# An instruction scheduler that models the vector engines' queues, in a one-layer hybrid decoder step

## The chip, the cores and the metric

The kernel runs on one core of one Trainium2 chip. The metric is the device time of one execution in microseconds (us), given as the median of several runs. One core has a matrix engine (TensorE, in the profile PE; PEld is its weight load), a vector engine (VectorE, DVE), an activation engine (ScalarE, ACT), a general engine (GpSimd, POOL) and a queue that issues transfers (SyncE, SP). Each engine works through its own instructions in the order in which the program lists them, and instructions on different engines wait for each other by semaphores.

## The reference

The reference is one step of one decoder layer for a prompt group (512 tokens) and a sample group (8 sequences of 8 tokens with 1024 cached positions each). Both share the weights.

```
h = rmsnorm(x, norm1_w)
rq, rk, rv, rg, aq, ak, av = split(h @ w_in)          # 7 sections of 512 columns
ro = silu(rg) * (groupnorm(retention(rq, rk, rv, state)) * gn_w + gn_b)
ao = dilated_attention(aq, concat(cache_k, ak), concat(cache_v, av))   # softmax, 8 heads of 64
x  = x + concat(ro, ao) @ w_out
h  = rmsnorm(x, norm2_w)
ua, ub = split(h @ w_up)                              # 2 x 2816 columns
x  = x + (silu(causal_conv3(ua)) * ub) @ w_down
y  = rmsnorm(x, normf_w)
```

It also returns the retention states, the new key and value windows and the convolution states of both groups. All arrays are float32.

## The kernel before, in words

All 576 tokens (512 prompt, 64 sample) are kept transposed, with the model's 1024 columns on partitions in 8 tiles. A dense layer is computed in chunks of 128 output columns. A chunk is 8 steps of 6 matmuls: activations and weights are split into a high and a low part (`xhi`/`xlo`, `whi`/`wlo`), three products are summed, and each covers the 576 tokens in two halves of 288. ScalarE makes `whi` from the loaded `wraw` (line 219), VectorE makes `wlo` (line 229), and `dense` (lines 245 to 261) issues the steps (line 254).

There are three stretches. In the first, the inputs are transposed and normalised and the retention heads run beside the input projection. In the middle one, after retention has ended, both attentions run beside what is left of the input projection. In the last one come the output projection and the gated convolution FFN.

The order of the instructions is made by the program itself, when it is built. Each part of the work is a Python generator, a stream. `Merge` (lines 96 to 143) keeps a clock in modelled nanoseconds of TensorE. A stream issues some instructions and then yields `(c0, c1)`: how long TensorE will be busy with them, and how long from then on the stream is not to be resumed (a guess written by hand at each yield, for the work of the other engines). It may yield `None` when it can't go on. Streams with a `left` (an estimate of their TensorE time still to come) share the matrix engine in proportion, by a virtual time `vt`; a third number in the yield is charged in place of `c0`. Streams without `left` go first whenever their time has come. There are three with `left` in the middle stretch: `in_proj` (the input projection), `attn_prompt` and `attn_sample`.

The middle stretch in detail. A head pair `hp` (0 to 3) needs the chunks of sections 5 (keys), 4 (queries) and 6 (values) of the input projection; `in_post` multiplies each finished chunk by `rstd_b` (lines 557 and 563) and transposes keys and values (`natural`, line 496). After all head pairs come four chunks of section 3, the gates (line 527).

`attn_prompt` starts four units per head pair (`attn_unit`), with at most two in flight: scores (lines 766 to 771), bias and minimum on VectorE (779), exponential on ScalarE (786), reciprocal of the sum on VectorE (789), scaling on GpSimd (791), transposes of the scaled weights (797), copies out of PSUM (801), product with the values (810).

`attn_sample` runs eight units, two per head pair, each of four sequences. Before a unit, the keys of each sequence are transposed (`keys`, lines 883 and 884, six transposes and two copies). When all four are there and the head pair's sections are there, GpSimd copies the new tokens' keys in (line 982) and `unit` is started: scores (893), bias and minimum (900), exponential (905), reciprocal and scaling (907, 908), transposes (916, 917), copies (920, 921), product with the cached values (928), copy (937), transpose (943), copies into `aoT` (946). Cached values lie in six buffers: after the third key of the next unit the stream waits for the current unit to have used its values (`while len(V) > 5`, line 975).

PSUM is shared: four small tiles `m` and two large tiles `d`. `room(n)` and `give(n)` count the small tiles in use; `give` frees them at once when the reading instruction has been issued. The large tiles are used by `in_proj` for its chunks and by `unit`, twice, for scores and for transposes. Nothing in the program counts them; a matmul that writes to a tile whose last reader has not finished waits on the engine. The input projection waits for the attention in one place (line 582): a chunk of head pair 2 or 3 is started only when all six attention units of head pair 0 or 1 are done.

Of the kernel before, what the change touches and what calls it, by code (L numbers as in the profile page):

```python
# [10 lines left out]
F32 = mybir.dt.float32  # L11
# [3 lines left out]
OP = mybir.AluOpType  # L15
# [3 lines left out]
P = 128  # L19
D = 1024  # L20
NP = 512
# [4 lines left out]
TS = 8  # L26
# [66 lines left out]
    return {"c_ident": ident.astype(f), "c_small": small, "c_kdec": kdec, "c_pbias": pb, "c_sbias": sb.astype(f)}  # L93


class Merge:


# [2 lines left out]

    def __init__(self):
        self.clock, self.live, self.n = 0.0, [], 0

    def floor(self):
        return min([e["vt"] for e in self.live if e["left"] and not e["stuck"]], default=0.0)

    def add(self, gen, left=None, delay=0.0):  # L110
        self.n += 1
        self.live.append({"g": gen, "left": left, "vt": self.floor(), "at": self.clock + delay, "n": self.n,
                          "stuck": False})

    def run(self, until=None):
        while self.live and not (until and until()):
            free = [e for e in self.live if not e["stuck"]]
            assert free, "every stream waits"
            ok = [e for e in free if e["at"] <= self.clock]
            if ok:  # L120
                e = min(ok, key=lambda e: (e["left"] is not None, e["vt"] if e["left"] else e["at"], e["n"]))
            else:
                e = min(free, key=lambda e: (e["at"], e["n"]))
                self.clock = e["at"]
            try:
# [12 lines left out]
            self.clock += c[0]  # L138
            e["at"] = self.clock + c[1]
            if e["left"]:  # L140
                p = c[2] if len(c) > 2 else c[0]
                e["vt"] += p / e["left"]
                e["left"] = max(e["left"] - p, 2000.0)
# [2 lines left out]
@with_exitstack  # L146
def decoder_step(ctx, tc, a):
    nc = tc.nc
    pe, dve, act, pool, sp = nc.tensor, nc.vector, nc.scalar, nc.gpsimd, nc.sync
# [11 lines left out]

    def room(n):

        while held[0] + n > 4:
            yield None
        held[0] += n

    def give(n):
        held[0] -= n

    def dtile():
        return psd.tile([P, 1024], F32, name="d", tag="d")

    def f32(ap):
        return ap.bitcast(F32)
# [149 lines left out]
    def halves():  # L325
        return [(h2, slice(h2 * 64, h2 * 64 + 64)) for h2 in range(2)]

    mg = Merge()
# [193 lines left out]
    def in_post(m, ps):  # L522
        sec, hp = m // 4, m % 4
        y = tok(ps)
        if sec == 3:
            t = atp.tile([P, T], F32, name="t3", tag="t6", bufs=1)
            dve.tensor_mul(t, y, rstd_b)
            yield 0.0, 800.0
            act.activation(t, t, AF.Silu)
            yield 0.0, 1700.0  # L530
            while ret_done[0] <= hp:
                yield None
            (dve if hp == 3 else pool).tensor_tensor(roT[:, hp], roT[:, hp], t, op=OP.mult)
            ready.add(hp)
        elif sec < 4:
            while sec == 1 and hp not in kready:
                yield None
            r = R.setdefault(hp, {})
            t = rp.tile([P, T], F32, name=f"r{sec}", tag=f"r{sec}", bufs=2)
            dve.tensor_mul(t, y, kds.pop(hp) if sec == 1 else rstd_b)  # L540
            if m in first:
                evac.append(m)
            while not psm:
                yield None
            yield 0.0, 700.0
            if sec in (1, 2):
                n = rp.tile([P, 5, P], F32, name=f"n{sec}", tag=f"n{sec}", bufs=2)
                yield from natural(t, n, slice(0, NS))
                r["kv"[sec - 1]] = n
            if sec == 1 and hp < 3:  # L550
                mg.add(load_kdec(hp + 1))
            r[sec] = t
        else:
            r = A.setdefault(hp, {})
            t = atp.tile([P, T], F32, name=f"t{sec}", tag=f"t{sec}", bufs=1 if sec == 6 else 2)
            if sec == 4:
                dve.scalar_tensor_tensor(t, y, -(DH ** -0.5), rstd_b, op0=OP.mult, op1=OP.mult)  # L557
                yield 0.0, 2300.0
                for h2, q in halves():
                    pool.tensor_copy(qbs[hp % 2][q, :, h2 * TS:(h2 + 1) * TS],  # L560
                                     t[q, NP:].rearrange("p (b t) -> p b t", b=B))
            else:
                dve.tensor_mul(t, y, rstd_b)
                yield 0.0, 1700.0
                n = atp.tile([P, 5, P], F32, name=f"n{sec}", tag=f"n{sec}", bufs=1 if sec == 5 else 2)
                if sec == 6:
                    pool.memset(n[:NS, 4], 0.0)
                yield from natural(t, n, UP)
                if sec == 6:
                    r["v"] = n  # L570
            r[sec] = t
            if sec > 4:
                yield 0.0, 3100.0
                store_window(n, "k" if sec == 5 else "v", hp)

    def in_proj():
        for m in IN_ORDER:
            sec, hp = m // 4, m % 4
            if m in first:
                ps = first[m]  # L580
            else:
                while hp > 1 and (sec < 3 and ret_done[0] < hp - 1 or sec > 3 and used.get(hp - 2, 0) < 6):
                    yield None
                ps = dtile()
                for c in dense(ps, ("in", m, 0), xhis, xlos, 0, KD, True, True):
                    yield c
                    if m == IN_ORDER[-1]:
                        last_in.append(1)
# [155 lines left out]
    def attn_unit(hp, i):  # L744
# [42 lines left out]
        yield 0.0, 600.0  # L787
        for ps, s, c in S:
            dve.reciprocal(c[:, 2:3], c[:, 1:2])  # L789
        for ps, s, c in S:  # L790
            pool.tensor_scalar(s[:, :n], s[:, :n], c[:, 2:3], 1.0, op0=OP.mult, op1=OP.mult)  # L791
        yield 0.0, 2.5 * n + 300.0
        yield from room(2)
        for ps, s, c in S:
            ps = mtile()
# [60 lines left out]
    def attn_sample():  # L856
# [19 lines left out]
        def keys(u, x):  # L876
            hp, g = units[u]
            b = 4 * g + x
            kt = kvb[0].tile([P, SK], F32, name="kt", tag="kt", bufs=5)
            for w in range(2):  # L880
                ps = mtile()
                for j in range(3):
                    pe.transpose(ps[:, j * P:(j + 1) * P], K[u, x][:, 3 * w + j], ident)  # L883
                (act.copy if w else dve.tensor_copy)(kt[:, w * 384:w * 384 + 384], ps[:, :384])  # L884
            del K[u, x]
            KT[u, x] = kt

        def unit(u):
            hp, g = units[u]
            ps = dtile()  # L890
            for n0, n1_ in ((0, 512), (512, SK)):
                for x in range(4):
# [2 lines left out]
            for x in range(4):  # L895
# [3 lines left out]
            c = kvb[0].tile([P, 4], F32, name="ssc", tag="ssc", bufs=2)  # L899
            dve.tensor_tensor_reduce(out=s[:, :SK], in0=ps[:, :SK], in1=SB[hp], scale=1.0, scalar=3e38, op0=OP.add,  # L900
                                     op1=OP.min, accum_out=c[:, 0:1])
            if g == 1 and hp < 3:
                load_bias(hp + 1)
            yield 0.0, 700.0
# [6 lines left out]
                              s[:, None, KEYS:SK].to_broadcast([P, B, TS]),  # L911
                              mine[:, g, :, None].to_broadcast([P, B, TS]), op=OP.mult)
            yield 0.0, 1100.0
            ps = dtile()
            for j in range(6):
                pe.transpose(ps[:, j * P:(j + 1) * P], s[:, j * P:(j + 1) * P], ident)
# [2 lines left out]
            pt = kvb[0].tile([P, 7, P], F32, name="spt", tag="spt", bufs=1)  # L919
            dve.tensor_copy(pt[:, :3].rearrange("p j q -> p (j q)"), ps[:, :384])  # L920
            act.copy(pt[:, 3:7].rearrange("p j q -> p (j q)"), ps[:, 384:KEYS + P])
            yield 0.0, 2200.0
            yield from room(1)
            ps = mtile()
# [42 lines left out]
        for u in range(8):  # L967
            hp, g = units[u]
            for x in range(4):
                yield from room(2)  # L970
                keys(u, x)
                give(2)
                yield 660.0, 1600.0
                ahead(4 * u + x + 4, "k")
                while len(V) > 5:
                    yield None
# [13 lines left out]
    fin_ret = []  # L990

# [28 lines left out]

    mg.add(mix_split())
    mg.run()
    mid.close()


# [306 lines left out]
```

## Time and profile before

| what | value |
|---|---|
| median of 3 runs | 830.26 us (829.99 to 830.6) |
| profiled execution, device time | 830.02 us |
| its span, first to last instruction | 828.2 us |
| PE busy | 809.3 us (98%) |
| PEld busy | 772.3 us (93%) |
| DVE, ACT, POOL busy | 413.4, 294.4, 148.0 us |
| granted TensorE clock | 0.997 of full speed |

A matmul's record lasts from its start to its last result, and the next one starts before that; so neighbouring matmuls overlap in the trace, and a PE that is shown busy may still have lost a fraction of a matmul. An engine's idle time before an instruction is put down to what ended it: another engine's instruction, a transfer, or "issue", where the profile shows nothing that it waited for.

### The profile page before, as it was taken

The numbers are of one execution on the slowest core, as the hardware profiler recorded it, in microseconds if no ns is written. First come the engines' busy times: TensorE is split into PE (matmuls) and PEld (weight loads), VectorE is DVE, ScalarE is ACT, GpSimd is POOL, SyncE is SP. The second block draws the span as 40 slices with busy tenths as digits, with TensorE's granted clock in tenths as the row PEclk, the third lists the DMA queues.
The fourth block names the chain that finished last, engine by engine and source line by source line (L and its number), as shares of the span: only waits on it lengthen the run. The fifth ranks groups of instructions, "written<-read, shape, count | busy, mean of one in ns | idle before, by whom it ended". The sixth has DMA issues, their size and how long they took to land.

```text
span 828.2 us, 15913 instructions
## 1 busy us (share of the span) xinstructions
PE 809.3 (98%) x6559; PEld 772.3 (93%) x6559; DVE 413.4 (50%) x792; ACT 294.4 (36%) x503; POOL 148.0 (18%) x240
## 2 busy tenths in 40 slices
PE   7999999999999999999999999999999999999995
PEld 5999999887887888999999999999999999999995
DVE  4664555665546566743545545432245545443333
ACT  5422222454535567433223323311123323332222
POOL 1321202111110213032122322100012322310111
PEclk9999999999999999999999999999999999999998
DMA  9354753678786863456255554443334455543213
GB/s 265 105 175 115 213 173 101 184 210 226 213 254 185 228 177 91 111 185 197 77 179 178 178 187 160 124 137 91 96 99 161 145 153 179 172 160 93 71 52 115
DMA packets 179798, 128.67 MB, mean 155 GB/s; under 512 B 14976, under 2 KB 176400, under 8 KB 179213
## 3 DMA queue, kind: packets, MB, share of 16 engines
q1 hardware_dynamic: 178573, 93.75, 40.4%
q10 hardware_dynamic: 928, 33.63, 11.3%
q8 instruction: 52, 0.85, 0.4%
q0 software_dynamic: 224, 0.28, 0.1%
q14 instruction: 21, 0.17, 0.1%
HBM read 121.52 MB, written 39.66 MB: 195 GB/s over the span
## 4 chain that ended last, share of the span: by engine, by line
PE 93%; ACT 3%; DVE 1%; issue 1%; DMA 1%; POOL 0%; SPq 0%; ACTq 0%; DVEq 0%
PE d L254 74%; PE m L883 2%; PE d L451 2%; PE m L928 1%; PE d L893 1%; PE m L810 1%; PE m L797 1%; PE m L496 1%; PE m L1222 1%; PE px L254 1%; PE m L666 1%; DMA wraw<-in_w_in_dram 1%; ACT s L786 1%; PE m L630 1%; PE px L410 1%
## 5 line engine op out<-in xcount | busy, mean ns | idle before, releaser
L219 ACT ACTIVATE whi<-wraw 128x1024 fp32r<-128x1024 f32 (+2 forms) x114 | 110.5, 970 | 369.2 <-issue 182.6
L229 DVE TENSOR_TENSOR wlo<-wraw,whi 128x1024 fp32r<-128x1024 f32 (+2 forms) x114 | 127.1, 1115 | 121.7 <-ACT whi L219 118.9
L254 PE MATMUL d<-bhi,whi 128*128 128x288 f32 x768 | 172.7, 306 | 1.2 <-DVE t L557 1.2
L254 PE MATMUL d<-bhi,wlo 128*128 128x288 f32 x768 | 164.2, 295 | 0.0
L254 PE MATMUL d<-blo,whi 128*128 128x288 f32 x768 | 163.9, 295 | 0.0
L254 PE MATMUL d<-hhi,whi 128*128 128x288 f32 x704 | 151.0, 296 | 0.0
L254 PE MATMUL d<-hlo,whi 128*128 128x288 f32 x704 | 150.8, 296 | 0.0
L254 PE MATMUL d<-hhi,wlo 128*128 128x288 f32 x704 | 150.7, 296 | 0.0
L254 PEld LDWEIGHTS d<-bhi,whi 128*128 128x128 f32 x768 | 121.7, 189 | 6.3 <-issue 3.1
L254 PEld LDWEIGHTS d<-bhi,wlo 128*128 128x128 f32 x768 | 123.3, 188 | 0.0
L254 PEld LDWEIGHTS d<-blo,whi 128*128 128x128 f32 x768 | 123.2, 188 | 0.0
L254 PEld LDWEIGHTS d<-hhi,whi 128*128 128x128 f32 x704 | 113.5, 189 | 0.1
L254 PEld LDWEIGHTS d<-hhi,wlo 128*128 128x128 f32 x704 | 113.5, 189 | 0.0
L254 PEld LDWEIGHTS d<-hlo,whi 128*128 128x128 f32 x704 | 113.5, 189 | 0.0
L1130 DVE TENSOR_TENSOR ue<-d,rstd_b 128x512 f32<-128x512 f32 x22 | 15.2, 691 | 74.5 <-PE d L254 74.5
L1149 POOL TENSOR_TENSOR g<-g,cv 128x512 f32<-128x512 f32 x20 | 25.8, 1289 | 142.2 <-DVE g L1146 136.7
L791 POOL TENSOR_SCALAR s<-s,sc 128x128 f32<-128x128 f32 (+3 forms) x32 | 17.3, 549 | 140.5 <-DVE sc L789 125.9
L1046 POOL TENSOR_TENSOR acc<-acc,sq 128x576 f32<-128x576 f32 x13 | 20.9, 1611 | 104.2 <-ACT sq L1045 104.2
L1135 POOL COPY cout<-ue 128x2 f32<-128x2 f32 x22 | 5.7, 260 | 137.6 <-DVE ue L1130 137.6
L884 ACT COPY kt<-m 128x384 f32<-128x384 f32 x32 | 15.3, 479 | 38.4 <-PE m L883 36.2
L883 PE MATMUL m<-ident,kc 128*128 128x128 f32 x192 | 27.4, 277 | 0.8 <-DVE sc L779 0.7
L884 DVE COPY kt<-m 128x384 f32<-128x384 f32 x32 | 17.8, 556 | 19.4 <-PE m L883 19.0
(269 smaller groups left out, 1027.3 us busy)
## 6 DMA issues: line engine op xcount, KB each, us to landing
wraw<-in_w_up_dram SPq DMA_DIRECT2D x44, 512.0 KB, 4.7
wraw<-in_w_in_dram SPq DMA_DIRECT2D x26, 512.0 KB, 3.8
kc<-in_cache_win_k_dram SPq DMA_DIRECT2D x32, 256.0 KB, 4.8
vc<-in_cache_win_v_dram SPq DMA_DIRECT2D x32, 256.0 KB, 3.2
wraw<-in_w_down_dram SPq DMA_DIRECT2D x16, 384.0 KB, 4.0
wraw<-in_w_down_dram SPq DMA_DIRECT2D x16, 320.0 KB, 3.2
kc<-in_cache_win_k_dram SPq DMA_DIRECT2D x64, 64.0 KB, 3.4
vc<-in_cache_win_v_dram SPq DMA_DIRECT2D x64, 64.0 KB, 3.3
```

What stands on the lines that cost most here:

```text
L219: act.activation(split[i][0][:, c], raw[i][:, c], AF.Copy)
L229: dve.tensor_sub(lo[:, c], raw[i][:, c], f32(hi[:, c]))
L254: pe.matmul(ps[:, C0 + s * H2:C0 + (s + 1) * H2], wt[:, rows[k] if rows else k - k0], x[k][:, s * H2:(s + 1) * H2], start=first and k == k ...
L410: pe.transpose(ps[:, s], xn[:r, j, k * P:(k + 1) * P], ident[:r, :r])
L451: pe.matmul(ps[i][:, C0 + s * H2:C0 + (s + 1) * H2], wt[:, k], x[k][:, s * H2:(s + 1) * H2], start=k == 0 and wt is hi and x is xhis, stop ...
L496: pe.transpose(p1[:, j * P:(j + 1) * P], src[:, j * P:(j + 1) * P], ident)
L791: pool.tensor_scalar(s[:, :n], s[:, :n], c[:, 2:3], 1.0, op0=OP.mult, op1=OP.mult)
L883: pe.transpose(ps[:, j * P:(j + 1) * P], K[u, x][:, 3 * w + j], ident)
L884: (act.copy if w else dve.tensor_copy)(kt[:, w * 384:w * 384 + 384], ps[:, :384])
L1046: pool.tensor_tensor(acc, acc, sq, op=OP.add)
L1130: dve.tensor_mul(u[:, 2:NP + 2], ya[:, :NP], rstd_b[:, :NP])
L1149: eng.tensor_tensor(g[:, :NP], g[:, :NP], c[:, :NP], op=OP.mult)
```

## The change

The diff adds a model of the three vector engines (`Queues`): each instruction issued through a small proxy (`Engine`) adds its modelled time to its engine's clock, and `queues.end` is when the last engine that the current step has used will be done. In the middle stretch alone (`mg.follow`), a stream other than `in_proj` is not resumed before `queues.end + 150`; small PSUM tiles count as free only at the modelled end of their reader; and `droom` lets a stream take a large tile only when the last but one that was taken has been read by the model.

Besides, of the two heads of an `attn_unit` one is now scaled by VectorE and not both by GpSimd; the four key steps of a sample unit are charged 1685 each (before, 660 each and 4100 after the unit's start); and the new tokens' keys of a sequence are copied as soon as its keys are transposed, where they are there already (`new_keys`). In `unit` and `in_post` the diff adds `dgive(ps)` behind each instruction that reads a large tile.

```diff
+class Queues:
+    COST = {"dve": (130.0, 1.1), "act": (150.0, 0.87), "pool": (250.0, 1.0)}
+    def __init__(self):
+        self.clock = dict.fromkeys(self.COST, 0.0)
+        self.now, self.end = 0.0, 0.0
+    def step(self, now):
+        self.now, self.end = now, now
+    def note(self, name, op, out):
+        base, each = self.COST[name]
+        n = math.prod(out.shape[1:])
+        if name == "pool" and op == "tensor_tensor":
+            each = 2.4
+        t = max(self.clock[name], self.now) + base + n * each
+        self.clock[name] = t
+        self.end = max(self.end, t)
+class Engine:
...
+            r = f(*args, **kw)
+            self.queues.note(self.name, op, kw["out"] if "out" in kw else args[0])
+            return r
...
@@ Merge.run @@
+            self.queues.step(self.clock)
             try:
                 c = next(e["g"])
...
             e["at"] = self.clock + c[1]
+            if self.follow and not e["dense"]:
+                e["at"] = max(e["at"], self.queues.end + 150.0)
@@ decoder_step @@
     def room(n):
-        while held[0] + n > 4:
-            yield None
+        while True:
+            while freed and freed[0][0] <= mg.clock:
+                held[0] -= freed.pop(0)[1]
+            if held[0] + n <= 4:
+                break
+            yield (0.0, max(freed[0][0] - mg.clock, 10.0)) if freed else None
         held[0] += n
     def give(n):
-        held[0] -= n
+        if mg.follow:
+            freed.append((queues.end, n))
+            freed.sort()
+        else:
+            held[0] -= n
+    large, read = [], {}
+    def dgive(ps):
+        read[id(ps)] = queues.end
+    def droom():
+        while mg.follow and len(large) > 1:
+            t = read.get(id(large[-2]))
+            if t is not None and t <= mg.clock:
+                break
+            yield None if t is None else (0.0, max(t - mg.clock, 10.0))
     def dtile():
-        return psd.tile([P, 1024], F32, name="d", tag="d")
+        large.append(psd.tile([P, 1024], F32, name="d", tag="d"))
+        return large[-1]
@@ in_proj; unit (before the scores and before the transposes) @@
+                yield from droom()
                 ps = dtile()
@@ attn_unit @@
-        for ps, s, c in S:
-            pool.tensor_scalar(s[:, :n], s[:, :n], c[:, 2:3], 1.0, op0=OP.mult, op1=OP.mult)
-        yield 0.0, 2.5 * n + 300.0
+        for eng, (ps, s, c) in zip((pool, dve), S):
+            eng.tensor_scalar(s[:, :n], s[:, :n], c[:, 2:3], 1.0, op0=OP.mult, op1=OP.mult)
+        yield 0.0, 1.25 * n + 500.0
@@ keys, new_keys @@
             KT[u, x] = kt
+            if hp in A and 5 in A[hp]:
+                new_keys(u, x)
+        def new_keys(u, x):
+            hp, g = units[u]
+            b = 4 * g + x
+            if (u, x) not in early:
+                early.add((u, x))
+                pool.tensor_copy(KT[u, x][:, KEYS:], A[hp][5][:, NP + b * TS:NP + (b + 1) * TS])
@@ attn_sample @@
-                yield 660.0, 1600.0
+                yield 660.0, 1600.0, 1685.0
...
             for x in range(4):
-                b = 4 * g + x
-                pool.tensor_copy(KT[u, x][:, KEYS:], A[hp][5][:, NP + b * TS:NP + (b + 1) * TS])
+                new_keys(u, x)
             flying["s"] += 1
             mg.add(unit(u), None, 600.0)
-            yield 0.0, 1000.0, 4100.0
+            yield 0.0, 1000.0
...
-    mg.add(in_proj(), 130.0e3)
+    mg.add(in_proj(), 130.0e3, dense=True)
...
     rpx.close()
+    mg.follow = True
...
     mg.run()
+    mg.follow = False
+    held[0] = 0
```

## Rows read from the trace of the kernel before

**Rows 1.** The profile's page: busy time by engine, and 40 slices.

```profile
PE 809.3 (98%) x6559; PEld 772.3 (93%) x6559; DVE 413.4 (50%) x792; ACT 294.4 (36%) x503; POOL 148.0 (18%) x240
...
PEld 5999999887887888999999999999999999999995
```

**Rows 2.** Busy time by stretch: window, its length, PE, PEld, DVE, ACT, POOL.

```profile
147.00:333.30 186.30, 182.28 (x1813) 157.86 (x1812) 109.71 (x279) 101.19 (x237) 29.13 (x76) 1.00 0.70 196
...
500.00:600.00 100.00, 100.00 (x754) 100.00 (x753) 36.52 (x47) 22.96 (x30) 8.22 (x12) 1.00 0.40 122
```

**Rows 3.** Waits of the weight load, 147 to 333.3 us: total, times, longest.

```profile
PEld d L893 <- issue: 4.2, 17, 0.3
...
PEld d L893 <- POOL kt L982: 2.1, 3, 1.5
PEld m L797 <- POOL s L791: 1.9, 7, 0.5
PEld m L883 <- DVE sc L779: 1.7, 4, 0.9
...
PEld d L254 <- DVE t L557: 1.5, 1, 1.5
...
PEld m L769 <- DVE kt L884: 0.7, 1, 0.7
...
PEld m L810 <- ACT ob L937: 0.2, 1, 0.2
```

**Rows 4.** The chain that ended last, around 186 us: start, us, what.

```profile
186.73 1.13 POOL kt L982
```

**Rows 5.** Groups of instructions by line: count, busy us, mean ns.

```profile
L883 PE MATMUL m<-ident,kc 128*128 128x128 f32 x192 | 27.4, 277 | 0.8 <-DVE sc L779 0.7
...
L229 DVE TENSOR_TENSOR wlo<-wraw,whi 128x1024 fp32r<-128x1024 f32 x13 | 16.3, 1255 | 2.2 <-ACT whi L219 2.0
...
L791 POOL TENSOR_SCALAR s<-s,sc 128x128 f32<-128x128 f32 (+3 forms) x32 | 17.3, 549 | 140.5 <-DVE sc L789 125.9 <-PE d L916 11.7 <-PE m L771 2.8
...
L908 DVE TENSOR_SCALAR ss<-ss,ssc 128x776 f32<-128x776 f32 x8 | 5.0, 625 | 0.3
...
L786 ACT ACT_TABLE_LOAD x2 | 2.6, 1283 | 0.0
```

**Rows 6.** The chain that ended last, where sample units meet the input projection.

```profile
197.78 1.01 PE m L928 x32
...
200.28 0.81 PE m L883 x6
201.09 0.79 PE d L254 x6
...
204.19 1.44 PE d L893 x16
205.63 0.99 PE d L254 x6
...
207.00 0.66 PE m L883 x6
...
216.29 1.67 PE m L928 x56
...
237.67 0.81 PE m L883 x6
...
250.59 1.44 PE d L893 x16
...
285.85 0.81 PE m L883 x6
...
294.87 1.44 PE d L893 x16
...
333.16 0.11 PE m L943
```

**Rows 7.** VectorE in order of time, the last gate chunk.

```profile
337.51 0.76 DVE L527 TENSOR_TENSOR t<-d,rstd_b 128x576 f32<-128x576 f32 x1
```

More of the change, by code (lines that the diff above doesn't have):

```diff
@@ L93, in _constants, with __init__, __getattr__, call @@
     return {"c_ident": ident.astype(f), "c_small": small, "c_kdec": kdec, "c_pbias": pb, "c_sbias": sb.astype(f)}
+class Queues:
[14 more added lines that the diff above has]
+class Engine:
+    def __init__(self, engine, name, queues):
+        self.engine, self.name, self.queues = engine, name, queues
+    def __getattr__(self, op):
+        f = getattr(self.engine, op)
+        if op == "dma_start":
+            return f
+        def call(*args, **kw):
+            r = f(*args, **kw)
+            self.queues.note(self.name, op, kw["out"] if "out" in kw else args[0])
+            return r
+        return call
 class Merge:
-    def __init__(self):
+    def __init__(self, queues):
         self.clock, self.live, self.n = 0.0, [], 0
+        self.queues, self.follow = queues, False
     def floor(self):
         return min([e["vt"] for e in self.live if e["left"] and not e["stuck"]], default=0.0)
-    def add(self, gen, left=None, delay=0.0):
+    def add(self, gen, left=None, delay=0.0, dense=False):
         self.n += 1
         self.live.append({"g": gen, "left": left, "vt": self.floor(), "at": self.clock + delay, "n": self.n,
-                          "stuck": False})
+                          "stuck": False, "dense": dense})
     def run(self, until=None):
@@ L148, in decoder_step @@
     nc = tc.nc
-    pe, dve, act, pool, sp = nc.tensor, nc.vector, nc.scalar, nc.gpsimd, nc.sync
+    pe, sp = nc.tensor, nc.sync
+    queues = Queues()
+    dve, act, pool = (Engine(e, n, queues) for e, n in ((nc.vector, "dve"), (nc.scalar, "act"), (nc.gpsimd, "pool")))
     ctx.enter_context(tc.manual_schedule())
@@ L162, in room @@
     def room(n):
-        while held[0] + n > 4:
-            yield None
+        while True:
[4 more added lines that the diff above has]
+            yield (0.0, max(freed[0][0] - mg.clock, 10.0)) if freed else None
         held[0] += n
+    freed = []
     def give(n):
-        held[0] -= n
+        if mg.follow:
[12 more added lines that the diff above has]
+            yield None if t is None else (0.0, max(t - mg.clock, 10.0))
     def dtile():
-        return psd.tile([P, 1024], F32, name="d", tag="d")
+        large.append(psd.tile([P, 1024], F32, name="d", tag="d"))
+        return large[-1]
     def f32(ap):
@@ L326, in halves @@
         return [(h2, slice(h2 * 64, h2 * 64 + 64)) for h2 in range(2)]
-    mg = Merge()
+    mg = Merge(queues)
     xhi = big.tile([P, KD, T], F32R, name="bhi", tag="bhi", bufs=1)
@@ L527, in in_post @@
             dve.tensor_mul(t, y, rstd_b)
+            dgive(ps)
             yield 0.0, 800.0
@@ L540, in in_post @@
             dve.tensor_mul(t, y, kds.pop(hp) if sec == 1 else rstd_b)
+            dgive(ps)
             if m in first:
@@ L557, in in_post @@
                 dve.scalar_tensor_tensor(t, y, -(DH ** -0.5), rstd_b, op0=OP.mult, op1=OP.mult)
+                dgive(ps)
                 yield 0.0, 2300.0
@@ L563, in in_post @@
                 dve.tensor_mul(t, y, rstd_b)
+                dgive(ps)
                 yield 0.0, 1700.0
@@ L886, in keys @@
             KT[u, x] = kt
+            if hp in A and 5 in A[hp]:
+                new_keys(u, x)
+        early = set()
+        def new_keys(u, x):
[4 more added lines that the diff above has]
+                pool.tensor_copy(KT[u, x][:, KEYS:], A[hp][5][:, NP + b * TS:NP + (b + 1) * TS])
         def unit(u):
             hp, g = units[u]
+            yield from droom()
             ps = dtile()
@@ L901, in unit @@
                                      op1=OP.min, accum_out=c[:, 0:1])
+            dgive(ps)
             if g == 1 and hp < 3:
@@ L913, in unit @@
             yield 0.0, 1100.0
+            yield from droom()
             ps = dtile()
@@ L921, in unit @@
             act.copy(pt[:, 3:7].rearrange("p j q -> p (j q)"), ps[:, 384:KEYS + P])
+            dgive(ps)
             yield 0.0, 2200.0
```

## The prediction

> **What bounds the kernel now.** I read the page's busy times first, then busy times by stretch, then what the matrix engine's weight load waits for, and last the chain that ended last. On the page PE is busy for 98% of the span and no other engine for more than 50% [rows 1], so PE sets the time. The slices of the weight load tell where it is not fed: 7 and 8 in the middle stretch, 9 from there to the last slice [rows 1]. Only the middle stretch, 147 to 333.3 us, is issued otherwise after the change, so only it can gain. There PE is idle for 186.30 - 182.28 = 4.0 us [rows 2]. That is too little, since a matmul's record reaches over the start of the next: six transposes take 0.66 us one behind the other (0.11 each), or 0.81 with a change of kind, and are recorded with 0.277 each [rows 5, 6], 0.17 more. A wait of up to 0.17 us thus leaves no gap.
>
> The weight load shows these waits. In this stretch it waited 27 times for a vector engine, in 15 kinds of which [rows 3] have the first five and the last: 10.4 us in all. Less 27 x 0.17 us that the matmuls still running cover, 5.8 us of PE time are lost. So the recoverable time lies between 4.0 (seen gaps) and 10.4 us (every wait in full); I take 5.8. The reader is to see who is waited for: copies of keys and scalings on POOL, readers of PSUM tiles on DVE and ACT [rows 3]. PE stands behind an instruction that was put into its list too early, while dense steps that need nothing stand behind it.
>
> **The change part by part.** *Waiting by the model (`follow`, `room`, `droom`).* It moves PE's instructions, and removes and adds none. The waits for a small tile's reader (L883 for L779 and the like) and for a large tile (L254 for L557, 1.5 us) [rows 3] are those that `room` and `droom` look at; the waits for scores, exponentials and copies are those that `follow` looks at. Its costs fit: by the diff a scaling of 776 elements on DVE is 130 + 854 = 984 ns, where 625 was measured, and `wlo` 1256 where 1255 was [rows 5]. It errs in three places. In a key step the two copies are counted from the step's start, while the six transposes ahead of them need 0.66 to 0.81 us, so those tiles count as free that much too early. Table loads on ACT (1.28 us each [rows 5], two before exponentials) are not counted. And the dense stream's own weight split is not waited for. I let 1.2 of the 5.8 us stand for these: -4.6 us. Bounds: 0 (every wait comes back at another place) to -10.4.
>
> *Early copies and split scaling.* The clearest case: at 186 us PE's scores of unit 1 stand behind four key copies on POOL, and these behind a scaling on POOL; the chain goes through POOL from 186.73 on for 1.13 us [rows 4], and the weight load lost 2.1 us in 3 waits of this kind and 1.9 in 7 for the scaling itself [rows 3]. Both are within the 5.8 us already. The price: 16 scalings move to DVE. Its nearest row is 625 ns for 776 elements [rows 5], an upper bound for 128 to 512, so at most 16 x 0.63 = 10 us on an engine with 186.3 - 109.7 = 76.6 us to spare [rows 2]; POOL loses 16 x 0.549 = 8.8 us. DVE's idle time hides it. If that cover were gone, what is queued behind a moved scaling would be the second head's copy and the key copies, at most 0.63 us later each time. I cost it at nothing.
>
> *Even pace of the keys.* It moves key steps against dense steps. Per unit the charge is the same (4 x 660 + 4100 = 6740 = 4 x 1685), but a unit starts only when all of it is charged; before, 4100 were charged later. It changes how often PE goes from dense steps to other work and back. A dense step of six takes 0.79 us in a run and 0.99 where it stands alone between kinds [rows 6], 0.2 us for an isolated step. By the code's order some 13 chunks, 104 dense steps, fall into the stretch; if 25 more or 15 fewer stood alone, that is +5 or -3 us. I take +0.3.
>
> *What the added waits make late.* The sample units form a chain of their own: with six value buffers the fourth key step of unit u+1 waits for unit u's product with the values, so unit follows unit at some 18.5 us (197.78 to 216.29 [rows 6]). Everything that `follow` and `droom` add lies on this chain. By the costs in the diff, waiting after the scores' minimum grows from 700 to 134 + 1000 = 1134 ns, and after the scaling from 1100 to about 1465: +0.8 us. On top comes what stands in the queue, at most one `wlo` (1.26 us) at each of the two: up to +2.5. And `droom` looks at the last tile but one in order of taking. When `in_proj` has taken a tile just before the unit took one for its scores, the unit's transposes now wait for the end of that chunk, though the unit's own first tile is free: between 0 and eight steps of 0.79, 6.3 us. Bounds are +0.8 and +9.6 us a unit; I take +2.5, for the code's own delays between scores and transposes (1500 + 600 + 700 + 2000 + 1100 ns) let most of a chunk go by. The stalls that go shorten the chain by 4.6 / 8 = 0.6, so 1.9 remain.
>
> Who waits for that chain? The chunk of head pair 2 waits for unit 1: its value product ends at 200.28 and the next dense step starts at 201.09 [rows 6], with no slack. Units 0 and 1 are late by 3.8 us in all, and in that time PE has head pair 1's prompt units to do; I count a quarter as idle, +1.0. Further on there is slack. Unit 2 starts 204.19 - 200.28 = 3.9 us after unit 1 has used its values, but unit 4 only 250.59 - 237.67 = 12.9 and unit 6 294.87 - 285.85 = 9.0 us after theirs [rows 6]: these two wait for the input projection, with 9.0 and 5.1 us to spare. The last unit's transpose is at 333.16 [rows 6], while the last gate chunk is read at 337.51 [rows 7]: 4.3 us. Two units late by 1.9 each fit into all three. So +1.0, bounds 0 and the rival below.
>
> **The sum.** Profiled execution 830.0 (0.2 below the median of the runs shown): 830.0 - 4.6 + 0.3 + 1.0 = 826.7 us.
>
> A rule gives another price. The Trainium skill, "Perfetto Trace Analysis", section "Identifying the Most-Contended Engine", says that matmul busy time tells little of TensorE's headroom and that the busy share of weight loads does. By it the stretch has 186.3 - 157.9 = 28.4 us of room where the dense stretch has none (100.00 of 100.00) [rows 2], and the sum could reach 802. The rows speak against most of that: the largest entry, 4.2 us at L893 in 17 waits, waits for nothing that the profile shows [rows 3], and there a load of 32 columns stands before a matmul of up to 512, so that the load is idle while the matmul is not.
>
> **The rivals.** *All waits go and nothing comes back.* For it: the modelled durations are those of the trace, and dense steps are there to fill. 830.0 - 5.8 = 824.2, down to 819.6 if every wait counts in full. Against it: the three gaps in the model. *The change does not do what it says:* it leaves about as many waits as it removes, since a queue model with hand-set delays beside it shifts PE's instructions against each other, and the delays before were long already (2000 ns after the exponential, 2200 after the copies). Then 829 to 831.5. *The sample chain becomes the bound* (slower): if a unit is late by x net, the first gate costs a quarter of 2x, unit 6 costs 2x - 5.1 and the end 2x - 4.3. At x = 3.1 this is 1.5 + 1.1 + 1.9 = 4.5 us and eats the gain of 4.3; that is the point from which it decides. At x = 4.5, where `droom` holds most units for half a chunk or more, it is 2.3 + 3.9 + 4.7 = 10.9: 830.0 - 4.6 + 0.3 + 10.9 = 836.6. For it: the chain has no slack at its first gate, and the added delays are never negative. Against it: 5 to 9 us of slack later. *The room of the weight loads:* 802 to 819.
>
> **How the numbers follow.** A difference of 0.2% (1.7 us) is about what can be told from no change here. The forecast (-1.7 to -5) gets 0.42, all waits gone 0.15, the weight loads' room 0.01: faster 0.58. No net effect gets 0.22. The sample chain as the bound gets 0.20, of which 0.12 lie below 833.5. The range runs from 822.5 (0.08 below it, half of the second case and the last) to 833.5 (0.08 above); the likeliest case alone is 825 to 828.5.
>
> **What would show it.** Right: between 147 and 333 us the weight load's waits for POOL, DVE and ACT fall from 10.4 to about 3 us, PE's idle time to about 1.5, and the output projection starts 3 us earlier. Early copies right: no score matmul waits for POOL. Chain right: the distance of two units' value products is 20 us or a little more; dense steps pause for some us before head pair 2's first chunk. Wrong: the weight load's waits stay near 10 us under other names; or PE is idle for several us in one piece, before head pair 2's chunk or between the last gate chunk and the output projection; or unit follows unit at over 22 us. A change before 147 or after 340 us would contradict the whole reading, since that code is issued as before.

## The result and the profile after

The changed kernel takes 837.56 us (837.01 to 842.63, 6 runs), the kernel before 829.67 us beside it: a ratio of 1.011, interval 1.0088 to 1.0133. It is slower by 7.9 us; 826.7 was forecast. Of the rivals it is the third, the chain of sample units as the bound, which was priced at 836.6 and given 0.20.

The page of the profile after, busy times by engine (to be held against [rows 1]):

```profile
span 836.0 us, 15866 instructions
...
PE 809.0 (97%) x6559; PEld 772.4 (92%) x6559; DVE 416.1 (50%) x808; ACT 297.4 (36%) x505; POOL 142.1 (17%) x224
```

PE is as busy as before, 809.0 against 809.3 us, so the 7.8 us of span are idle time. Where they lie shows in two views. The tile `hhi`, which the FFN reads, is first used by a matmul at 387.8 us before and at 395.5 us after, 7.7 us later; the last stretch is as long as it was. Busy times by stretch after (window, length, PE, PEld, DVE, ACT, POOL, granted clock):

```profile
147.00:186.00 39.00, 39.00 (x353) 35.89 (x353) 23.28 (x60) 20.12 (x49) 4.86 (x16) 1.00 0.79 217
186.00:201.00 15.00, 12.50 (x153) 8.95 (x152) 10.12 (x28) 8.96 (x23) 1.24 (x3) 1.00 0.89 245
201.00:327.00 126.00, 121.70 (x1200) 106.66 (x1200) 71.14 (x192) 64.76 (x155) 15.16 (x40) 1.00 0.68 194
327.00:344.00 17.00, 11.45 (x133) 9.12 (x132) 9.74 (x17) 11.49 (x18) 2.52 (x4) 0.91 0.11 32
```

PE's idle time is 0 + 2.5 + 4.3 + 5.55 = 12.35 us, against 4.0 before [rows 2]. The first two windows before were:

```profile
147.00:186.00 39.00, 37.98 (x343) 33.50 (x342) 23.39 (x63) 21.20 (x53) 4.39 (x11) 1.00 0.74 206
186.00:201.00 15.00, 14.41 (x166) 11.84 (x165) 7.67 (x14) 5.24 (x11) 3.39 (x13) 1.00 0.87 239
```

So the first 39 us are 1.0 us better than before, the 15 us at the first gate 1.9 us worse, and the end is open. The weight load's waits after, 147 to 345 us (total, times, longest), answer to [rows 3]:

```profile
PEld m L876 <- POOL s L131: 3.7, 2, 2.7
...
PEld d L1009 <- DVE ss L131: 2.0, 2, 1.2
...
PEld m L1022 <- DVE spt L131: 1.8, 1, 1.8
...
PEld m L962 <- DVE sc L131: 1.2, 2, 0.9
...
PEld d L984 <- POOL kt L131: 0.3, 1, 0.3
```

L131 is the proxy through which all vector instructions now go, so one reads the tiles. The wait of the scores for key copies on POOL has gone from 2.1 to 0.3 us, as the early copies should make it. But all waits for POOL, DVE and ACT together are not fewer microseconds: 12.9 us in 17 waits, where there were 10.4 in 27. The largest entry is the transposes of a prompt unit that wait for their scaling on POOL (L876). At the end the transposes (L1009) and value products (L1022) of a sample unit wait for their own VectorE work, because PE has nothing else left. The chain that ended last, where [rows 6] have the first gate and the last unit:

```profile
188.04 0.82 PE m L962 x6
...
198.89 1.67 PE m L1022 x56
...
201.22 0.79 PE d L328 x6
...
331.07 1.09 PE m L876 x8
332.17 3.19 PE d L328 x24
335.36 1.05 PE m L889 x16
...
340.32 2.85 PE m L1022 x56
...
343.52 0.47 PE m L1037
343.99 8.02 PE d L328 x59
```

At the first gate dense steps pause until unit 1's values are used: the last before it is at 185.9, the next at 201.22, only 0.1 us later than before (201.09 [rows 6]). At the end the four dense steps at 332.17 are the last of the input projection. VectorE reads the last gate chunk at 335.46, and the last unit's transpose comes at 343.52: an open end of 8 us, where [rows 6, 7] had 4.3 us of cover. Three pieces of VectorE in order of time are these, the read of the last gate chunk, the last unit's scaling and the copy of its result (columns as in [rows 7]):

```profile
335.46 0.76 DVE L131 TENSOR_TENSOR t<-d,rstd_b 128x576 f32<-128x576 f32 x1
...
336.99 0.62 DVE L131 TENSOR_SCALAR ss<-ss,ssc 128x776 f32<-128x776 f32 x1
...
344.03 0.39 DVE L131 COPY aoT<-m 64x32 f32<-64x32 f32 x2 [3.76 <-PE m L1037]
```

How the chain of units fell behind: PE in order of time, first score matmuls of units 4 to 6 (units 4 to 6 before: 250.52, 270.85 and 294.80):

```profile
249.09 1.51 PE L984 MATMUL d<-kt,qb 128*32 128x512 f32 x16
...
282.47 1.51 PE L984 MATMUL d<-kt,qb 128*32 128x512 f32 x16
...
299.40 1.51 PE L984 MATMUL d<-kt,qb 128*32 128x512 f32 x16
```

Unit 7 starts at 327.36 after and 314.01 before. From unit 4 to unit 7 a unit takes (327.4 - 249.1) / 3 = 26.1 us, before (314.0 - 250.5) / 3 = 21.2. Up to unit 4 nothing is lost; the last three lose 4.9 us each on average, but unevenly: the steps are 33.4, 16.9 and 28.0 us, where they were 20.3, 24.0 and 19.2.

What comes late in the long steps are the keys. The last three key steps of unit 5, after and then before:

```profile
255.49 0.82 PE L962 MATMUL m<-ident,kc 128*128 128x128 f32 x6
...
269.62 1.16 PE L962 MATMUL m<-ident,kc 128*128 128x128 f32 x6 [0.56 <-DVE sc L131]
...
278.92 0.82 PE L962 MATMUL m<-ident,kc 128*128 128x128 f32 x6
```

```profile
257.32 0.82 PE L883 MATMUL m<-ident,kc 128*128 128x128 f32 x6
...
260.79 0.87 PE L883 MATMUL m<-ident,kc 128*128 128x128 f32 x6
...
267.11 0.89 PE L883 MATMUL m<-ident,kc 128*128 128x128 f32 x6
```

### The profile page after: what moved, and what is told of

Its sections match the earlier page's. It is cut to its first block, busy times and chain, and to the rows that moved or that the text cites. A ratio compares the mean times of both kernels' runs of the same rounds, so it can differ in the third digit from the quotient of the medians.

```text
span 836.0 us, 15866 instructions
## 1 busy us (share of the span) xinstructions
PE 809.0 (97%) x6559; PEld 772.4 (92%) x6559; DVE 416.1 (50%) x808; ACT 297.4 (36%) x505; POOL 142.1 (17%) x224
## 4 chain that ended last, share of the span: by engine, by line
PE 93%; DVE 3%; ACT 2%; DMA 1%; issue 0%; POOL 0%; SPq 0%; ACTq 0%; DVEq 0%; POOLq 0%
PE d L328 73%; PE m L962 2%; PE d L525 2%; PE m L1022 2%; PE m L889 1%; PE d L984 1%; PE m L570 1%; PE m L876 1%; PE m L1318 1%; ACT s L131 1%; PE px L328 1%; PE m L745 1%; DMA wraw<-in_w_in_dram 1%; PE m L848 1%; DVE wlo L131 1%; PE m L709 1%
## 5 line engine op out<-in xcount | busy, mean ns | idle before, releaser
L131 ACT ACTIVATE whi<-wraw 128x1024 fp32r<-128x1024 f32 (+2 forms) x114 | 110.5, 970 | 365.9 <-issue 186.6
L131 DVE TENSOR_TENSOR wlo<-wraw,whi 128x1024 fp32r<-128x1024 f32 (+2 forms) x114 | 126.8, 1112 | 125.5 <-ACT whi L131 122.8
L131 POOL TENSOR_TENSOR g<-g,cv 128x512 f32<-128x512 f32 (+1 forms) x40 | 31.2, 802 | 142.1 <-DVE g L131 136.7
L131 DVE TENSOR_TENSOR ue<-d,rstd_b 128x512 f32<-128x512 f32 (+1 forms) x44 | 18.1, 453 | 74.6 <-PE d L328 74.6
L131 POOL COPY cout<-ue 128x2 f32<-128x2 f32 (+1 forms) x44 | 30.8, 730 | 137.8 <-DVE ue L131 137.8
L131 DVE TENSOR_TENSOR xT<-d,xT 128x576 f32<-128x576 f32 x23 | 17.4, 758 | 53.8 <-PE d L328 53.7
L131 POOL TENSOR_TENSOR acc<-acc,sq 128x576 f32<-128x576 f32 x13 | 21.0, 1612 | 109.0 <-ACT sq L131 109.0
L131 DVE SCALAR_TENSOR_TENSOR cv<-ue,vec,cv 128x592 f32<-128x592 f32 x44 | 36.5, 829 | 0.8
L131 ACT COPY kt<-m 128x384 f32<-128x384 f32 x32 | 15.3, 477 | 52.9 <-PE m L962 52.0
L131 POOL TENSOR_SCALAR s<-s,sc 128x128 f32<-128x128 f32 (+3 forms) x16 | 10.5, 655 | 131.1 <-DVE sc L131 123.6
```

What stands on the lines that cost most here:

```text
L131: r = f(*args, **kw)
```

## The experiments

Each run's ratio is to the kernel before on the same chip. "Cover" is how long after the last sample unit's transpose VectorE reads the last gate chunk, from the starts of the two instructions in the traces (4.5 us for the kernel before, where the pieces of the chain gave 4.3); negative is an open end.

| run | us | ratio (interval) | last unit's scores at | cover |
|---|---|---|---|---|
| before | 829.67 | | 314.0 | 4.5 |
| the change | 837.56 | 1.011 (1.0088 to 1.0133) | 327.4 | -8.0 |
| e1 old charges | 834.65 | 1.0049 (1.0031 to 1.0067) | 324.8 | -7.9 |
| e2 charges alone | 833.14 | 1.0038 (1.0025 to 1.0051) | 317.2 | 4.5 |
| e3 no droom | 832.69 | 1.0026 (1.0013 to 1.0038) | 321.2 | -3.4 |
| e4 split, early | 833.96 | 1.0046 (1.0031 to 1.0061) | 317.6 | 6.0 |
| e5 same order | 831.14 | 1.0012 (1.0002 to 1.0023) | 315.4 | 4.5 |
| e6 one delay | 830.67 | 1.0006 (0.9995 to 1.0017) | 314.9 | 4.6 |
| e7 one share | 830.29 | 1.0006 (0.9994 to 1.0018) | 313.3 | 4.5 |
| e8 no droom, old charges | 836.67 | 1.0077 (1.0062 to 1.0093) | 333.2 | -11.7 |
| e9 no room | 829.23 | 0.9993 (0.9978 to 1.0008) | 314.7 | 1.3 |
| e10 room alone | 858.92 | 1.0353 (1.0337 to 1.0368) | 353.8 | -36.3 |
| e11 follow alone | 829.09 | 0.9990 (0.9980 to 1.0000) | 316.7 | -2.8 |
| e12 room, keys free | 829.70 | 0.9991 (0.9982 to 1.0000) | 313.3 | 4.0 |
| e13 follow, old charges | 829.94 | 0.9990 (0.9980 to 0.9999) | 318.7 | -2.8 |
| e14 follow only | 831.10 | 1.0015 (1.0006 to 1.0023) | 315.5 | 3.6 |
| e15 change, keys free | 829.19 | 0.9995 (0.9983 to 1.0007) | 318.9 | 0.3 |

**First question: the charges, or the model's waits?** e1 puts the old charges into the change, e2 the new ones into the kernel before, e3 takes the wait for large tiles out of the change, e4 puts the split scaling and the early copies alone into the kernel before.

```diff
# e1 (e2 is the reverse, in the kernel before)
-                yield 660.0, 1600.0, 1685.0
+                yield 660.0, 1600.0
...
-            yield 0.0, 1000.0
+            yield 0.0, 1000.0, 4100.0
# e3
     def droom():
-        while mg.follow and len(large) > 1:
+        while False:
```

> The change with the sample stream's charges as before (660 a key step, 4100 after the unit's start). Two theories. Pace: with 4 x 1685 a unit starts only when all of it is charged, so by the shares each unit, the last one too, starts later against the input projection, and the last 8 us of the stretch lie open. Waits: the waits of the queue model (room, droom, follow) stretch the chain of sample units. Pace expects the whole loss gone here: 825 to 830 us, the last unit's scores no later than 316 us. Waits expects 834 to 838 us and an open end as in the change.

> The kernel before with nothing but the new charges (1685 a key step, none after the unit's start). Pace expects 834 to 840 us, with idle time of PE before the output projection. Waits expects 829 to 831 us, since nothing waits for the model.

> The change without the wait for large tiles (droom returns at once; a matmul on a tile still being read then waits on the engine, as before). Waits, if droom is the largest part of it, expects 829 to 833 us and a unit that follows a unit 2 to 4 us sooner. Pace expects 836 to 839 us, as the change.

> The kernel before with only the split scaling and the early key copies; no queue model, old charges. Both theories expect no loss: 827.5 to 830 us, with the 2.1 us of weight-load waits for the key copies on POOL gone and most of the 1.9 us for the scaling. If the scaling on DVE is itself what holds the chain, it is slower than before by over 1 us.

Neither theory held in all four: the times that Waits expects came out in e1 and e3, but e2 and e4 contradict both. The charges are not the open end: with the old ones it is as open as in the change (e1), and with the new ones alone it is covered (e2). The wait for large tiles looked like the cause in e3, but e2 and e4, where nothing waits for a model and the end is covered, cost 3 to 4 us too, and the parts did not add up.

**Second question: does any new order cost that much?** e5 is e4 with the old delay behind the scaling, so PE's order is that of before and only the work of other engines moves. e6 and e7 change no work, only a number of the scheduler. e8 is e1 without the wait for large tiles.

```diff
# e5: as e4, but
         for eng, (ps, s, c) in zip((pool, dve), S):
             eng.tensor_scalar(s[:, :n], s[:, :n], c[:, 2:3], 1.0, op0=OP.mult, op1=OP.mult)
         yield 0.0, 2.5 * n + 300.0
# e6 (unit, behind the exponential)
-            yield 0.0, 2000.0
+            yield 0.0, 2100.0
# e7
-    mg.add(in_proj(), 130.0e3)
+    mg.add(in_proj(), 127.0e3)
```

> The kernel before with the split scaling and the early key copies, but with the old delay after the scaling (2.5 n + 300), so that PE's instructions stand in exactly the order of before. Two theories for the 3 to 4 us that single parts cost. Order: the order of before is a favourable one among its neighbours, and whatever shifts it costs that, while the work on other engines is harmless or helps. Parts: the scaling on VectorE is itself late for what waits on it. Order expects 826.5 to 830 us and the weight load's waits for POOL nearly gone; Parts expects 832 to 834 us, as with the new delay.

> The kernel before with one delay of the sample unit set from 2000 to 2100 ns (after its exponential): no work changed, PE's order shifted from the middle of the stretch on. Order expects 831 to 834 us, about what each part of the change cost. Parts expects 829.5 to 831 us.

> The kernel before with the input projection's share set from 130 to 127 (thousand): again no work changed, PE's order shifted in some places. Order expects 831 to 834 us; Parts expects 829.5 to 831 us.

> The change with the old charges and without the wait for large tiles; the rest of the queue model, the split scaling and the early copies stay. If the wait for large tiles makes the open end, as its removal alone suggested, the last unit's transpose stands within 3 us of the last gate chunk's read and the time is 829 to 833 us. If the other waits (small tiles, resuming at the queues' end) make it, 834 to 837 us.

Small shifts of the order cost at most what can be measured (e6, e7), so an order is not slower for being new; that theory fell for small shifts (e2 and e4 move more). e5 shows what becomes of a wait that is taken away. Its weight-load waits, 147 to 333.3 us:

```profile
PEld m L883 <- DVE sc L779: 2.6, 4, 1.2
...
PEld d L254 <- DVE t L557: 2.0, 1, 2.0
...
PEld m L797 <- POOL s L791: 0.7, 2, 0.4
```

The key copies are gone from the list and the scaling has gone from 1.9 to 0.7 us, 3.3 us less for the two. But the waits for PSUM tiles have grown from 1.7 to 2.6 and from 1.5 to 2.0 [rows 3], all waits for vector engines together have only gone from 10.4 to 9.8, and the time is no better, 1.0012.

Since PE's order is the same, the two traces can be compared matmul by matmul. Ahead of unit 1's scores at 186 us e5 is 0.3 us earlier than the kernel before, behind them 1.45: taking the key copies out of the way did gain 1.1 us. At 231.8 us 0.5 of it is lost. A reader of a large tile (L557) now stands on VectorE behind a scaling that was moved there (L791), and PE waits for it; VectorE and PE in e5, and PE before:

```profile
230.56 0.49 DVE L791 TENSOR_SCALAR s<-s,sc 128x512 f32<-128x512 f32 x1
230.96 0.75 DVE L557 SCALAR_TENSOR_TENSOR t<-d,rstd_b 128x576 f32<-128x576 f32 x1
```

```profile
231.77 0.53 PE L254 MATMUL d<-bhi,whi 128*128 128x288 f32 x2 [1.75 <-DVE t L557]
```

```profile
232.64 0.53 PE L254 MATMUL d<-bhi,whi 128*128 128x288 f32 x2 [1.23 <-DVE t L557]
```

At 311.5 us another 0.6 us is lost in the same way: a moved scaling stands in front of the reader of a small tile (L779). Between the two PE loses 1.6 us that no wait shows, because the granted clock of this execution fell (windows and columns as above):

```profile
232.00:234.00 2.00, 2.00 (x11) 1.99 (x11) 0.33 (x2) 0.59 (x1) 0.82 (x6) 0.57 1.11 304
234.00:236.00 2.00, 2.00 (x12) 1.99 (x11) 1.54 (x2) 0.48 (x1) 0.00 (x0) 0.58 0.48 124
```

Four of e5's ten runs have a mean clock of 0.994, as this one; the median of the other six is 830.6 us, still no better than the 830.04 of the kernel before beside them.

e8 fell the other way from e3: without the wait for large tiles the end is more open, not less. So that wait isn't the cause, and what all the open ends so far had in common was the rest of the model.

**Third question: small tiles, or resuming at the queues' end?** e9 takes the modelled small tiles out of the change, e10 leaves only them of the model, e11 leaves only the resuming.

```diff
# e9, e11
     def give(n):
-        if mg.follow:
-            freed.append((queues.end, n))
-            freed.sort()
-        else:
-            held[0] -= n
+        held[0] -= n
# e10
-            if self.follow and not e["dense"]:
-                e["at"] = max(e["at"], self.queues.end + 150.0)
# e10, e11: droom as in e3
```

> The change with the small PSUM tiles given back at once, as before (give without the model); resuming at the queues' end, the wait for large tiles, the charges, the split scaling and the early copies stay. Two theories for the open end of the stretch, which the change and the runs with the modelled small tiles show, with and without the wait for large tiles. Room: small tiles that count as held until the modelled end of their reader starve the key steps, which need two of four, and so delay the chain of sample units. Follow: resuming each stream at the queues' end does it. Room expects the last gate chunk to be read no earlier than 1 us before the last unit's transpose, and 829 to 832.5 us; Follow expects 834 to 838 us with an open end.

> The change with the modelled small tiles as the only part of the model in force (no resuming at the queues' end, no wait for large tiles); charges, split scaling and early copies stay. Room expects the chain at its latest: the end open by 10 us or more and 838 to 845 us. Follow expects 831 to 834 us, what the other parts cost alone.

> The change with resuming at the queues' end as the only part of the model in force; charges, split scaling and early copies stay. Room expects 829 to 833 us and no open end; Follow expects 834 to 838 us with one.

The small tiles it is: without them the change costs nothing (0.9993), and alone they cost 29 us, more than was expected. e11 has an end open by 2.8 us and is not slower for it. PE in e10 in order of time, the key transposes from 286 us on:

```profile
288.26 0.88 PE L960 MATMUL m<-ident,kc 128*128 128x128 f32 x6
...
327.87 0.82 PE L960 MATMUL m<-ident,kc 128*128 128x128 f32 x6
...
334.72 2.48 PE L960 MATMUL m<-ident,kc 128*128 128x128 f32 x18
```

For 39.6 us no key step comes. From the start of unit 5 (292.0 us) on, two small tiles are all that the next one asks for; by the code a head pair's prompt output keeps one of the four for as long as its units run. The rest of the keys come when the prompt units are through (their last value product ends at 334.79) and the dense steps have been used up (the last gate chunk is read at 328.1).

**Fourth question: do the key steps starve, or does every step come late? And where did the gain go?** e12 is e10 with one exception: a key step counts tiles that wait for their modelled end as free. e15 makes the same exception in the whole change. e13 is e11 with the old charges; e14 is the kernel before with the resuming alone.

```diff
# e12, e15
-    def room(n):
+    def room(n, plain=False):
...
-            if held[0] + n <= 4:
+            if held[0] + n - (sum(x for _, x in freed) if plain else 0) <= 4:
                 break
...
-                yield from room(2)
+                yield from room(2, True)
                 keys(u, x)
```

> The run with the modelled small tiles alone, with one exception: a key step counts the tiles that wait for their modelled end as free, as before the change; all other steps ask the model. If the key steps' starving for two tiles is what delays the chain, nearly all of the 29 us come back: 829 to 834 us, the last unit's scores before 322 us. If the model delays every step alike (scores, transposes and value products of the units too), at least a third stays: 839 us or more.

> Resuming at the queues' end as the only part of the model, with the split scaling and the early copies, and the old charges. If the new charges start the last unit late even without the tile model, this is 1 to 2 us faster than with the new ones: 827 to 828.5 us. If the charges hardly matter: 828.5 to 830 us.

> The kernel before with resuming at the queues' end and nothing else of the change. The forecast's term for the waits that go was -4.6 us with the tile waits in it; if it holds for the part that follows the queues alone, 826 to 828.5 us and PE's idle time in the stretch at most 2.5 us. If each wait that goes comes back at the next place, 829 to 831 us and 3.5 to 5 us idle.

> The change whole, with the one exception that a key step counts the small tiles that wait for their modelled end as free. If the key steps' starving is the change's loss, it comes within 2 us of the kernel before, 828.5 to 832 us, with the last unit's scores before 319 us. If resuming at the queues' end and the wait for large tiles lose more together with the tile model than alone, 833 to 837 us stay.

With one line for the key steps the 29 us come back whole (858.92 to 829.70), and so does the loss of the change (837.56 to 829.19). In e12 the key transposes come as they did before; PE in order of time:

```profile
295.62 0.88 PE L960 MATMUL m<-ident,kc 128*128 128x128 f32 x6
298.53 0.82 PE L960 MATMUL m<-ident,kc 128*128 128x128 f32 x6
301.42 0.82 PE L960 MATMUL m<-ident,kc 128*128 128x128 f32 x6
308.81 0.87 PE L960 MATMUL m<-ident,kc 128*128 128x128 f32 x6
```

The charges make no difference once the tiles are right (e13 as e11). e14, e15 and e9 tell where the gain went. Busy times of 147 to 345 us, in this order (PE's busy time is the third number):

```profile
147.00:345.00 198.00, 193.76 (x1897) 168.58 (x1895) 117.91 (x295) 105.83 (x243) 29.51 (x78) 1.00 0.69 190
```

```profile
147.00:345.00 198.00, 192.87 (x1908) 169.87 (x1907) 123.84 (x312) 106.24 (x244) 22.79 (x63) 1.00 0.70 193
```

```profile
147.00:345.00 198.00, 194.27 (x1906) 169.89 (x1905) 125.47 (x312) 106.71 (x244) 24.18 (x63) 1.00 0.68 191
```

PE is idle for 4.2, 5.1 and 3.7 us; before it was 4.0 in the same stretch. No version beats the kernel before by more than can be told: the best, e11 and e13, have a ratio of 0.9990 with intervals that end at 1.0000 and 0.9999.

## Why the prediction was wrong

**What bounds the kernel: right.** PE sets the time, only the middle stretch changed (the FFN starts 7.7 of the 7.8 us later), and the chain of sample units is the thing next to the bound.

**The waits that go, -4.6 us: wrong in the sum.** Named waits went, but others came in their place, and PE's idle time stayed. The weight load's waits for POOL, DVE and ACT were to fall from 10.4 to about 3 us. They are 12.9 us in the change, and with the tiles mended still 9.9 (e9), 7.8 (e11), 7.7 (e12), 9.7 (e13) and 9.4 (e15), added up from 147 to 345 us. These versions gain 0.1 to 0.8 us (ratios 0.9990 to 0.9995) where 4.6 were counted. The working treated the 27 waits as independent terms to be added. e5 follows one of them: the key copies' wait did give its 1.1 us, and readers of PSUM tiles behind the moved scalings took as much back. What made the new waits in the other runs was not followed one by one. Why e14, the resuming alone, is even 0.15% slower than the kernel before was not settled.

**What the added waits make late, +1.0 us: the step that failed.** It counted `follow` and `droom` on the units' chain at +2.5 us a unit, and `room` only among the gains. But `room` lies on the same chain, in front of it: a key step asks for two of four small tiles at once, the streams without a share go first whenever their time has come, and with a tile held until the modelled end of its reader the key steps found none. e10 and e12 show it for the tile model alone, e15 for the change: with the key steps exempt, unit 5's last key comes at 262.5 and not at 278.9 us, and the loss of 7.9 us is gone. Whether it is the need of two tiles or the low priority that starves them was not separated. `droom`, which the working named as the large risk, is not it: e9 and e15 keep it and lose nothing, and e3 and e8 point opposite ways. The prediction had one sentence on what `room` gets wrong, that tiles count as free too early in a key step; what it did was the opposite, key steps that come too late.

**The size and the slack.** Units 5 to 7 lost 4.9 us each on average, not 1.9. The first gate cost PE 2.5 us of idle time between 186 and 201 us where it was 0.6 in the kernel before, so +1.9 against the +1.0 forecast. But units 0 and 1 were not late by 3.8 us there, since dense steps resume only 0.1 us later, and 1.0 us had been gained ahead of the gate. The slack of 4.3 us at the end was taken to hold two late units. The last unit's scores came 13.4 us later (327.4 against 314.0) and its transpose 10.4 (343.52 against 333.16), while the last gate chunk was read 2.0 us earlier. The rival's formula, with 4.9 in it, gives 0.5 x 4.9 + (9.8 - 5.1) + (9.8 - 4.3) = 12.7 us; measured were 1.9 at the gate, 5.55 at the end and 1.9 between, 9.3, less the 1.0 gained at the start. It named the right places, but it hung on `droom`, which is not the cause. That its 836.6 us comes within 1 us of the result is luck: it holds a gain of 4.6 us that did not come, and 10.9 us of loss where some 8.3 were measured.

**Early copies, split scaling: right for the key copies, not that the moved work costs nothing.** In e5 the waits for POOL go from 4.0 to 1.1 us; in the change they are 4.0 again, at the prompt units' transposes. e5 is 1.1 us slower than before, part of it by the clock. What is queued behind a moved scaling came some 0.5 us later, which the prediction had named and costed at nothing; but it was readers of PSUM tiles that PE waits for, and in two places this took back the 1.1 us that the early copies had gained. e4's loss of 3.8 us came with the new delay behind the scaling, since with the old delay it is not there; which wait of the new order makes it was not settled, nor was e2's loss of 3.2 us.

**The pace: +0.3 us by more isolated dense steps.** Not shown by itself. What the charges cost depends on the rest: nothing with the tile model out of the way (e11 and e13), 3.2 us alone (e2), and in the change, where the old ones leave 4.4 us of the loss (e1).

**The room of the weight loads (802 us): not borne out.** By the rule of the Trainium skill, "Perfetto Trace Analysis", section "Identifying the Most-Contended Engine", which judges TensorE's headroom by the busy share of weight loads, the estimate was 28 us; no version of the order came below 827.99 us in any run.

## What to carry to other kernels

When a scheduler gets a model of a resource, ask for each stream that takes it whether it still gets a turn: holding a resource longer here starved the stream that needs two pieces at once and comes behind others that keep asking, and that stream was the head of the longest chain. Waits of an in-order engine are not terms to be added: price what is late next, on the engine that the work moves to as well, and take the sum of waits as a bound, never as the gain. Where only other engines' work moves, lay the two traces on each other, instruction by instruction: that shows where a gain is lost again. And where filler work covers a chain's end, count how much is left when the last link starts, because every gap that filler closes early is taken from there.

## What the runs showed of the hardware

An open end costs more than its idle time. In the change, PE was busy for 1.62 of the 3.0 us from 335 us on and for 0.72 of the next 2.3 us, and then the granted clock fell: it was 0.57 on average from 340.3 to 343.5 us and 0.50 from there to 344 us, the lower of the two levels (1.2 GHz). The windows, columns as above:

```profile
335.00:338.00 3.00, 1.62 (x21) 1.24 (x20) 2.81 (x6) 1.88 (x4) 0.00 (x0) 1.00 0.01 3
338.00:340.30 2.30, 0.72 (x7) 0.48 (x5) 1.23 (x2) 0.99 (x2) 0.11 (x1) 1.00 0.03 7
340.30:343.50 3.20, 2.83 (x56) 2.38 (x56) 0.00 (x0) 0.89 (x3) 0.10 (x1) 0.57 0.53 164
343.50:344.00 0.50, 0.48 (x2) 0.48 (x3) 0.00 (x0) 0.50 (x2) 0.00 (x0) 0.50 0.00 0
```

The last unit's 56 value matmuls took 2.85 us there, against 1.67 for unit 1's at 198.89: 1.2 us that no idle time shows.

In e5 the fall came behind a single idle time, 1.75 us up to 231.77 us: the clock was 0.57 and 0.58 in the two windows from 232 to 236 us. The same wait of 1.23 us in the kernel before, and one of 2.21 us before the change's transposes at 331.07, were not followed by a fall.
